# First token mixer reordered: u over half of the contraction, then v, then the rest of u, from one pool of tiles; the first norm and the spreading of a column redone

## The chip, the core and the metric

The kernel runs on one core of a Trainium2 chip. Time is device microseconds (us) of that core, the median of the runs shown. Five engines run in order, each with its own instruction stream: TensorE (PE, the matrix multiplier; PEld is its weight load), VectorE (DVE), ScalarE (ACT), GpSimd (POOL) and SyncE (SP, which issues most of the transfers from HBM). They wait for each other through semaphores. A scheduler in the language orders each engine's stream when the kernel is built; pools of tiles decide which instruction has to wait for a buffer.

## What is computed

Two layers over a sequence of 256 rows of 2048 features. Layer 0 mixes tokens with a chunked gMLP, layer 1 with attention; each is followed by a ConvFFN. The change is in layer 0's mixer:

```python
mod = silu(c) @ w_ada[i] + b_ada[i]              # 6 vectors of 2048 for each layer
sh1, sc1, gt1, sh2, sc2, gt2 = split(mod)
h = rmsnorm(x, g_norm) * (1 + sc1) + sh1
z = gelu(h @ w_in); u, v = split(z)              # w_in is 2048 x 4096
v = rmsnorm(v, g_v)
sv = einsum("gij,njgc->nigc", w_s, v) + b_s      # 16 groups, 2 chunks of 128 rows
x = x + gt1 * ((u * sv) @ w_out)
```

## The kernel before

Everything is float32, and each matrix product is split in three: an operand is cast to a rounded part (`hi`, on ACT) and a rest (`lo`, on DVE), and PE adds up hi*hi, hi*lo and lo*hi. A weight block is 1 MB, [128 x 2048]; `weight()` loads it into one of five `raw` buffers, casts it in two halves (L186) and subtracts in two halves (L187), into five buffers each for hi and lo. One block gives PE 48 matmuls of 256 columns, or 24 of 512.

The modulation is not a matmul. `ada()` (L135 to L143) loads 1 MB of `w_ada`, one vector of 128 outputs, into one of the same five `raw` buffers, and one DVE instruction (L138) multiplies it by the spread condition `cond_bc` and sums it up. There are 192 of these in the program. `queue` holds them in the order in which they are needed; `need()` forces those that the next step wants, and `pump()` takes as many more for each weight block as `state["rate"]` says.

The first mixer (`gmlp`, L296) does this: `rstd_bcast` forms the reciprocal norm of each row of x, and spreads it over the partitions: DVE writes it into a diagonal matrix (`dg`, L252) which PE multiplies by ones. The v half of `w_in` then runs with the contraction outermost: for each of 16 blocks kb, two `ada` (SC1 and SH1 of kb), the weight block, the modulated input (`make_h`: `ht` and `hlo` on DVE, `hhi` on ACT), and 24 matmuls into eight PSUM banks `pv`. After it v is squashed and normed. The u half runs by output block: 16 blocks `pu`, each with the whole contraction, which needs all of h; two of them stand ahead of the gating matmuls `pg` (32 of 128x128, operands `ws` and `bs` of 1 MB each), 14 behind. Then 16 output blocks `po` with `w_out`, each followed by the residual (L292). The ConvFFN begins with a norm of the new x and its first matmuls `pfa`.

## Time and profile before

| | |
|---|---|
| median of 3 runs | 2160.53 us (2158.19 to 2160.58) |
| the profiled execution | 2160.85 us, of which 2158.9 us are its span |
| PE busy | 2086.4 us, 97% of the span |
| DVE busy | 1704.8 us, 79% |
| ACT busy | 1020.2 us, 47% |
| moved by DMA | 580.62 MB, mean 269 GB/s |
| granted TensorE clock, mean | 0.983 of full speed |

The span runs from the first instruction to the last. Busy time is the time in which an engine executes an instruction; matmuls overlap each other, so a busy PE is not yet a PE at its peak. A start-to-start distance within a stream of equal instructions is the pace of the engine.

### The profile page before, as it was taken

The page shows a single profiled execution, that of the slowest core. Times are in us where ns is not written, and L with a number is a line of the kernel's source. Part 1 is how long each engine was busy: PE and PEld are TensorE (multiplying, and loading weights), DVE is VectorE, ACT ScalarE, POOL GpSimd, SP SyncE. Part 2 cuts the span into 40 slices and gives each one's busy share as a digit, 9 for nine tenths or more (in the row PEclk, how much of TensorE's full clock was granted, in tenths as well). Part 3 has the DMA queues.
Part 4 walks back from the last instruction along what each step waited for, and adds up shares of the span by engine and source line. Part 5 has one row for each costly group of instructions (what it writes and reads, how often), then busy time and mean ns, then how long its engine had stood idle before and what let it go on. Part 6 is the DMA issues. An engine that isn't in the chain of part 4 may idle for free.

```text
span 2158.9 us, 39151 instructions
## 1 busy us (share of the span) xinstructions
PE 2086.4 (97%) x16328; PEld 2020.9 (94%) x16328; DVE 1704.8 (79%) x2291; ACT 1020.2 (47%) x1501; POOL 16.6 (1%) x15
## 2 busy tenths in 40 slices
PE   6889998999999999999999999899999999999997
PEld 4669998999999999999988789899999999999997
DVE  8989888899988989889985677876978666655665
ACT  3354443446544554345455554443753455434542
POOL 0000000000000000000000000000000000000000
PEclk8999999999999999999999999899999999999999
DMA  9999987995798889888966346578558655555542
GB/s 381 400 378 372 347 334 278 335 363 206 286 362 332 330 320 344 336 324 316 341 244 214 117 176 236 218 283 296 197 179 318 229 191 180 192 182 189 178 159 94
DMA packets 85137, 580.62 MB, mean 269 GB/s; under 512 B 9952, under 2 KB 11488, under 8 KB 25056
## 3 DMA queue, kind: packets, MB, share of 16 engines
q1 hardware_dynamic: 84960, 578.12, 72.0%
q8 instruction: 128, 2.10, 0.4%
q14 instruction: 49, 0.40, 0.0%
HBM read 575.99 MB, written 2.10 MB: 268 GB/s over the span
## 4 chain that ended last, share of the span: by engine, by line
PE 55%; issue 36%; DVE 7%; ACT 1%; POOL 0%; DMA 0%; SPq 0%; POOLq 0%; DVEq 0%; ACTq 0%
PE pf L203 18%; PE pd L203 11%; PE po L203 4%; PE pw L203 4%; PE pu L203 4%; PE pfc L203 4%; PE pk L203 3%; DVE ada L138 3%; PE pq L203 3%; DVE lo L187 2%; PE pfa L203 2%; PE pqo L507 1%; PE pv L203 1%; PE psc L478 0%; ACT hi L186 0%
## 5 line engine op out<-in xcount | busy, mean ns | idle before, releaser
L186 ACT CAST hi<-w 128x1024 fp32r<-128x1024 f32 x740 | 741.0, 1009 | 916.6 <-PE pf L203 348.5
L187 DVE TENSOR_TENSOR lo<-w,hi 128x1024 fp32r<-128x1024 f32 x740 | 857.9, 1169 | 329.9 <-ACT hi L186 326.3
L203 PE MATMUL pf<-hhi_f,hi 128*128 128x256 f32 x2144 | 604.4, 282 | 0.0
L203 PE MATMUL pf<-hhi_f,lo 128*128 128x256 f32 x2144 | 601.2, 280 | 0.0
L203 PE MATMUL pf<-hlo_f,hi 128*128 128x256 f32 x2144 | 600.9, 280 | 0.0
L138 DVE CUSTOM_DVE_ANT_0 ada<-ada,cond_bc,bada 128x2048 f32<-128x2048 f32 x192 | 449.2, 2345 | 42.6 <-DMA ada<-in_wada 42.5
L203 PEld LDWEIGHTS pf<-hlo_f,hi 128*128 128x128 f32 x2144 | 404.8, 189 | 0.0
L203 PEld LDWEIGHTS pf<-hhi_f,lo 128*128 128x128 f32 x2144 | 404.3, 189 | 0.0
L203 PEld LDWEIGHTS pf<-hhi_f,hi 128*128 128x128 f32 x2144 | 403.8, 188 | 0.0
L203 PE MATMUL pd<-fhi_f,lo 128*128 128x256 f32 x1408 | 394.7, 281 | 0.0
L203 PE MATMUL pd<-flo_f,hi 128*128 128x256 f32 x1408 | 393.3, 280 | 0.0
L203 PE MATMUL pd<-fhi_f,hi 128*128 128x256 f32 x1408 | 391.1, 279 | 0.0
L203 PEld LDWEIGHTS pd<-fhi_f,hi 128*128 128x128 f32 x1408 | 264.8, 189 | 0.0
L203 PEld LDWEIGHTS pd<-fhi_f,lo 128*128 128x128 f32 x1408 | 264.7, 188 | 0.0
L203 PEld LDWEIGHTS pd<-flo_f,hi 128*128 128x128 f32 x1408 | 264.6, 188 | 0.0
L203 PE MATMUL pfc<-hhi_f,hi 128*128 128x256 f32 x448 | 125.3, 281 | 0.0
L203 PE MATMUL pfc<-hlo_f,hi 128*128 128x256 f32 x448 | 125.0, 281 | 0.0
L203 PE MATMUL pfc<-hhi_f,lo 128*128 128x256 f32 x448 | 124.4, 281 | 0.0
L571 DVE SCALAR_TENSOR_TENSOR t<-pf,cw,t 128x255 f32<-128x255 f32 x240 | 101.7, 474 | 0.0
L203 PEld LDWEIGHTS pfc<-hlo_f,hi 128*128 128x128 f32 x448 | 84.2, 188 | 0.0
L203 PEld LDWEIGHTS pfc<-hhi_f,lo 128*128 128x128 f32 x448 | 84.2, 189 | 0.0
L203 PEld LDWEIGHTS pfc<-hhi_f,hi 128*128 128x128 f32 x448 | 84.1, 188 | 0.0
(187 smaller groups left out, 2838.3 us busy)
## 6 DMA issues: line engine op xcount, KB each, us to landing
ada<-in_wada SPq DMA_DIRECT2D x192, 1024.0 KB, 6.6
w<-in_wup SPq DMA_DIRECT2D x134, 1024.0 KB, 4.9
w<-in_wdn SPq DMA_DIRECT2D x64, 1024.0 KB, 4.9
w<-in_wup SPq DMA_DIRECT2D x48, 896.0 KB, 5.9
w<-in_wdn SPq DMA_DIRECT2D x32, 768.0 KB, 4.6
w<-in_wv SPq DMA_DIRECT2D x16, 1024.0 KB, 6.9
w<-in_wu SPq DMA_DIRECT2D x16, 1024.0 KB, 7.2
w<-in_wout SPq DMA_DIRECT2D x16, 1024.0 KB, 5.2
```

What stands on the lines that cost most here:

```text
L138: V.tensor_tensor_reduce(out=w, in0=w, in1=cond_bc, op0=ALU.mult, op1=ALU.add, scale=1.0, scalar=bada[:, l, m:m + 1], accum_out=mod[:, l, ...
L186: A.copy(hi[:, :n], w[:, c:c + n])
L187: V.tensor_tensor(out=lo[:, :n], in0=w[:, c:c + n], in1=hi[:, :n].bitcast(F32), op=ALU.subtract)
L203: T.matmul(out, lhsT=a, rhs=b, start=start, stop=stop, skip_group_check=True)
L507: T.matmul(po, lhsT=va[:, kc, g * P:(g + 1) * P], rhs=ps_[h][:, kc, :], start=kc == 0, stop=kc == TC - 1)
L571: V.scalar_tensor_tensor(out=o[:, to], in0=a[:, frm], scalar=cw[:, l, tap, n:n + 1], in1=o[:, to], op0=ALU.mult, op1=ALU.add)
```

## The change

The u half of `w_in` is cut in two along the contraction. The mixer now runs:

1. u over the contraction blocks 0 to 7, contraction outermost, into eight banks `pua` (each holds two output blocks). Each block still comes with two `ada` and one `make_h`. The eight banks are copied to SBUF by ACT (`us`).
2. v over all 16 blocks. h of blocks 0 to 7 is there; blocks 8 to 15 are made on the way, with `ada` pumped at a rate of `RV` = 1.1 for each block.
3. the other half of u, by output (`u_rest`, eight blocks of two outputs each, added to `us` by DVE); the gating matmuls stand behind four of them. The rate is `RG` = 0.5.
4. the output blocks, as before, with a rate of `RO` = 1.15 in place of 0.7.

The number of weight blocks, `ada` and matmuls stays. v, u, sv and y now come in tiles of 512 columns from one pool of 20 slots (`slot`), and `ws` and `bs` have tiles of their own and no longer take `raw` buffers. A column is spread by one matmul whose stationary operand repeats it (`spread`), in place of a diagonal matrix; all four later norms use it too. The first sum of squares is four wide squares and three adds. `ident`, `bada` and `gn` are issued from ACT's queue; `gf`, `gv`, `cw` and `cb` stand in `late()`, behind the first stage in the code. The h tiles of the two mixers lose their padding of 8 columns.

```diff
-RO = 0.7
+RO = 1.15
+RV = 1.1
+RG = 0.5
+SVAT = 4
+HS = 20
...
+    ident = small("ident", [P, P], ident_d, A)
     x = const.tile([P, NB, S], F32, tag="x", name="x")
     for j in range(0, NB, 4):
         Q.dma_start(x[:, j:j + 4, :], xT_d[:, j:j + 4, :])
-    gf = small("gf", [P, NB], gf_d)
-    gv = small("gv", [P, NB], gv_d)
-    cw = small("cw", [P, DEPTH, 3, 2 * NPAIR], cw_d)
-    cb = small("cb", [P, DEPTH, 2 * NPAIR], cb_d)
...
+    bada = small("bada", [P, DEPTH, 6 * NB], bada_d, A)
+    gn = small("gn", [P, DEPTH * 2, NB], gn_d, A)
...
-    for b in range(NB // 2):
+    def spread(out, col):
+
+        T.matmul(out, lhsT=col.broadcast_to([P, P]), rhs=ident, start=True, stop=True)
+
+    for b in range(NB // 4):
         pb = bank(f"cb{b}")
-        dg = tmp.tile([P, S], F32, tag="ht", name=f"dgc{b}")
-        for i in range(2):
-            j = 2 * b + i
-            V.tensor_scalar(out=dg[:, i * P:(i + 1) * P], in0=ident, scalar1=cond[:, j:j + 1],
-                            scalar2=None, op0=ALU.mult)
-        T.matmul(pb[:, :S], lhsT=ones, rhs=dg, start=True, stop=True)
-        A.copy(cond_bc[:, b * S:(b + 1) * S], pb[:, :S])
+        for i in range(4):
+            spread(pb[:, i * P:(i + 1) * P], cond[:, 4 * b + i:4 * b + i + 1])
+        A.copy(cond_bc[:, b * 512:(b + 1) * 512], pb)
...
-        dg = tmp.tile([P, S], F32, tag="ht", name=f"dg_{name}")
...
-                V.tensor_scalar(out=dg[:, t * P:(t + 1) * P], in0=ident, scalar1=r[:, t:t + 1],
-                                scalar2=None, op0=ALU.mult)
-                T.matmul(pr[:, t * P:(t + 1) * P], lhsT=ones, rhs=dg[:, t * P:(t + 1) * P], start=True, stop=True)
+                spread(pr[:, t * P:(t + 1) * P], r[:, t:t + 1])
...
+    def new_h(name, step=0):
+        hts["hi"] = hbuf.tile([P, NB, S + step], F32R, tag="hhi", name=f"hhi_{name}")[:, :, :S]
+        hts["lo"] = hbuf.tile([P, NB, S + step], F32R, tag="hlo", name=f"hlo_{name}")[:, :, :S]
...
+    def late():
+
+        for t, src in ((gf, gf_d), (gv, gv_d), (cw, cw_d), (cb, cb_d)):
+            Q.dma_start(t, src)
...
-            gm = phase(st, "gm", NB)
+            gm = phase(st, "gm", 1)
             R = rstd()
             hhi, hlo = new_h("a")
-            v = gm.tile([P, TC, D], F32, tag="v", name="v")
-            pv = [[bank(f"pv{t}_{n}") for n in range(4)] for t in range(TC)]
-            for kb in range(NB):
+
+            def slot(name, dtype=F32):
+
+                return gm.tile([P, 2 * S + STEP], dtype, tag="half", name=name, bufs=HS)[:, :2 * S]
+
+
+            def h_block(kb):
                 need(l, SC1, kb)
                 need(l, SH1, kb)
+
+
+            pu = [bank(f"pua{i}") for i in range(H)]
+            for kb in range(H):
+                h_block(kb)
+                w = weight(wu0_d[kb], 2048)
+                make_h("a", l, 0, R, kb)
+                for i in range(H):
+                    for s in range(2):
+                        prod_b(pu[i][:, s * S:(s + 1) * S], w((2 * i + s) * P, P), hhi[:, kb, :], hlo[:, kb, :],
+                               kb == 0 and s == 0, kb == H - 1)
+            us = [slot(f"us{i}") for i in range(H)]
+            for i in range(H):
+                A.copy(us[i], pu[i])
+            late()
+
+
+            pv = [[bank(f"pv{t}_{n}") for n in range(4)] for t in range(TC)]
+            state["rate"] = RV
+            for kb in range(NB):
+                if kb >= H:
+                    h_block(kb)
                 w = weight(wv_d[kb], 2048)
-                make_h("a", l, 0, R, kb)
+                if kb >= H:
+                    make_h("a", l, 0, R, kb)
                 for t in range(TC):
                     ts_ = slice(t * P, (t + 1) * P)
                     for n in range(4):
...
                         mm(pv[t][n], hhi[:, kb, ts_], w(n * 512, 512)[1], False, False)
                     for n in range(4):
                         mm(pv[t][n], hlo[:, kb, ts_], w(n * 512, 512)[0], False, kb == NB - 1)
-            state["rate"] = 1.0
+            state["rate"] = RG
...
-                    vs = v[:, t, n * 512:(n + 1) * 512]
-                    A.activation(vs, pv[t][n], AF.Gelu)
-                    s = gm.tile([P, 512], F32, tag="vsq", name=f"vsq{t}{n}", bufs=2)
-                    A.activation(s, vs, AF.Square, accum_out=ss[:, t, n:n + 1])
+                    A.activation(v[t][n], pv[t][n], AF.Gelu)
+                    A.activation(slot(f"vsq{t}{n}"), v[t][n], AF.Square, accum_out=ss[:, t, n:n + 1])
...
+            for n in range(4):
+                for t in range(TC):
...
+                    V.tensor_scalar(out=v[t][n], in0=v[t][n], scalar1=rv[:, t:t + 1], scalar2=None, op0=ALU.mult)
+            ws = gm.tile([P, D], F32, tag="ws", name="ws")
+            Q.dma_start(ws, wsT_d)
+            bs = gm.tile([P, D], F32, tag="bs", name="bs")
+            Q.dma_start(bs, bs_d.partition_broadcast(P))
...
+            def u_rest(i):
+
+                w = weight(wu1_d[i], 2048)
+                pb = bank(f"pub{i}")
+                for s in range(2):
+                    for k in range(NB - H):
+                        prod_b(pb[:, s * S:(s + 1) * S], w((s * (NB - H) + k) * P, P), hhi[:, H + k, :],
+                               hlo[:, H + k, :], k == 0 and s == 0, k == NB - H - 1)
+
+                def fin():
+                    V.tensor_tensor(out=us[i], in0=pb, in1=us[i], op=ALU.add)
+                    A.activation(us[i], us[i], AF.Gelu)
+                    if i in sv:
+                        y_of(i)
+
+                pend.append(fin)
...
+            def sv_of(i):
+
+                pg = bank(f"pg{i}")
+                sv[i] = slot(f"sv{i}")
...
+            def y_of(i):
+                V.tensor_tensor(out=us[i], in0=us[i], in1=sv[i], op=ALU.mult)
+                hi, lo = slot(f"yhi{i}", F32R), slot(f"ylo{i}", F32R)
+                A.copy(hi, us[i])
+                V.tensor_tensor(out=lo, in0=us[i], in1=hi.bitcast(F32), op=ALU.subtract)
+                for s in range(2):
+                    ys[2 * i + s] = (hi[:, s * S:(s + 1) * S], lo[:, s * S:(s + 1) * S])
+
+            for i in range(SVAT):
+                u_rest(i)
             flush()
-            ws = raw_tile("ws")
-            Q.dma_start(ws, wsT_d)
-            bs = raw_tile("bs")
-            Q.dma_start(bs, bs_d.partition_broadcast(P))
-            for g in range(NB):
-                gsl = slice(g * P, (g + 1) * P)
-                pg = bank(f"pg{g}")
-                for t in range(TC):
-                    T.matmul(pg[:, t * P:(t + 1) * P], lhsT=v[:, t, gsl], rhs=ws[:, gsl],
-                             start=True, stop=True)
-                V.scalar_tensor_tensor(
-                    out=v[:, :, gsl], in0=pg[:, :S].rearrange("p (t i) -> p t i", t=TC),
-                    scalar=gv[:, g:g + 1], in1=bs[:, gsl].unsqueeze(1).broadcast_to([P, TC, P]),
-                    op0=ALU.mult, op1=ALU.add)
-            sv_ready.append(True)
-            for j in range(2):
-                y_of(j, us[j])
-            for j in range(2, NB):
-                u_block(j)
+            for i in range(H):
+                sv_of(i)
+            for i in range(SVAT):
+                y_of(i)
+            for i in range(SVAT, H):
...
 
-    for j in range(NB):
-        square_into("mx0", j, x[:, j, :])
+    quads = []
+    for j in range(0, NB, 4):
+        q = los.tile([P, 4 * S], F32, tag="lo", name=f"quad{j}")
+        A.activation(q, x[:, j:j + 4, :].rearrange("p j t -> p (j t)"), AF.Square)
+        quads.append(q)
+    for a, b in ((0, 1), (2, 3), (0, 2)):
+        V.tensor_tensor(out=quads[a], in0=quads[a], in1=quads[b], op=ALU.add)
+    accs["mx0"] = [quads[0][:, k * S:(k + 1) * S] for k in range(4)]
     gmlp(0, lambda: rstd_bcast("mx0", True))
...
-    o["wu"] = _nblock(win[:, :D])
+    wu = win[:, :D].reshape(2, NB // 2, P, NB // 2, 2, P)
+    o["wu0"] = win[:D // 2, :D].reshape(NB // 2, P, D)
+    o["wu1"] = wu[1].transpose(2, 1, 3, 0, 4).reshape(NB // 2, P, D)
```

SP's queue at the start, before; `ada` and `w` are 1 MB each, `w<-in_wv` are weight blocks of v:

```order
L97 DMA x<-in_xT 128x1024 x4
L88 DMA gf<-in_gf 128x16
L88 DMA gv<-in_gv 128x16
L88 DMA cw<-in_cw 128x528
L88 DMA cb<-in_cb 128x176
L137 DMA ada_16_223<-in_wada 128x2048
L137 DMA ada_0_227<-in_wada 128x2048
L180 DMA w_230<-in_wv 128x2048
L137 DMA ada_17_268<-in_wada 128x2048
L137 DMA ada_1_272<-in_wada 128x2048
L180 DMA w_275<-in_wv 128x2048
```

The same place after; `w<-in_wu` are the blocks of u's first half:

```order
L99 DMA x<-in_xT 128x1024 x4
L139 DMA ada_16_177<-in_wada 128x2048
L139 DMA ada_0_181<-in_wada 128x2048
L182 DMA w_184<-in_wu 128x2048
L139 DMA ada_17_246<-in_wada 128x2048
L139 DMA ada_1_250<-in_wada 128x2048
L297 DMA gf<-in_gf 128x16
L297 DMA gv<-in_gv 128x16
L297 DMA cw<-in_cw 128x528
L297 DMA cb<-in_cb 128x176
L361 DMA ws<-in_wsT 128x2048
L363 DMA bs<-in_bs 128x2048
L182 DMA w_253<-in_wu 128x2048
```

`ws` and `bs`, which stood behind the 18th weight block, now stand ahead of the second one.

DVE in the first mixer, one contraction block before (`ISA` is the `ada` instruction and its read-out):

```order
L138 ISA ada_3_362,mod<-ada_3_362,cond_bc,bada 128x2048
L138 ISA mod 128x1
L142 SCALAR_TENSOR_TENSOR gs<-mod,gn 128x1
L275 SCALAR_TENSOR_TENSOR ht_a_375<-x,gs,R_mx_210 128x256
L187 TENSOR_TENSOR lo_0_368<-w_365,hi_0_367 128x1024
L187 TENSOR_TENSOR lo_1024_372<-w_365,hi_1024_371 128x1024
L278 SCALAR_TENSOR_TENSOR hlo_a<-ht_a_375,mod,hhi_a 128x256
L138 ISA ada_20_403,mod<-ada_20_403,cond_bc,bada 128x2048
L138 ISA mod 128x1
L138 ISA ada_4_407,mod<-ada_4_407,cond_bc,bada 128x2048
L138 ISA mod 128x1
L142 SCALAR_TENSOR_TENSOR gs<-mod,gn 128x1
```

and in the middle of v after:

```order
L140 ISA ada_9_870,mod<-ada_9_870,cond_bc,bada 128x2048
L140 ISA mod 128x1
L277 SCALAR_TENSOR_TENSOR hlo_a<-ht_a_1116,mod,hhi_a 128x256
L189 TENSOR_TENSOR lo_0_876<-w_873,hi_0_875 128x1024
L189 TENSOR_TENSOR lo_1024_880<-w_873,hi_1024_879 128x1024
L140 ISA ada_26_907,mod<-ada_26_907,cond_bc,bada 128x2048
L140 ISA mod 128x1
L144 SCALAR_TENSOR_TENSOR gs<-mod,gn 128x1
L274 SCALAR_TENSOR_TENSOR ht_a_1157<-x,gs,R_mx_165 128x256
L189 TENSOR_TENSOR lo_0_914<-w_911,hi_0_913 128x1024
L189 TENSOR_TENSOR lo_1024_918<-w_911,hi_1024_917 128x1024
L140 ISA ada_10_945,mod<-ada_10_945,cond_bc,bada 128x2048
```

Two `ada` for each pair of `lo` and one `ht` and `hlo` have become one `ada` for each pair, and one `ht` and `hlo` for two pairs.

DVE at the end of u's second half and the start of the output blocks, after; `us_733` to `us_736` are the last four u tiles, `ylo` is the rest part of their products, which the output matmuls read:

```order
L375 TENSOR_TENSOR us_736<-pub_1989,us_736 128x512
L189 TENSOR_TENSOR lo_0_2179<-w_2176,hi_0_2178 128x1024
L140 ISA ada_41_2238,mod<-ada_41_2238,cond_bc,bada 128x2048
L140 ISA mod 128x1
L189 TENSOR_TENSOR lo_1024_2183<-w_2176,hi_1024_2182 128x1024
L402 TENSOR_TENSOR us_735<-us_735,sv_1740 128x512
L405 TENSOR_TENSOR ylo_1920<-us_734,yhi_1919 128x512
L189 TENSOR_TENSOR lo_0_2244<-w_2241,hi_0_2243 128x1024
L140 ISA ada_42_2301,mod<-ada_42_2301,cond_bc,bada 128x2048
L140 ISA mod 128x1
L402 TENSOR_TENSOR us_736<-us_736,sv_1748 128x512
L189 TENSOR_TENSOR lo_1024_2248<-w_2241,hi_1024_2247 128x1024
L405 TENSOR_TENSOR ylo_1986<-us_735,yhi_1985 128x512
```

The adds, products and subtractions of the last u tiles stand between `lo` and `ada` of the output blocks.

## Rows read from the trace of the kernel before

**Rows 1.** Profile page, busy time of PE: us, share of the span, instructions.
```profile
PE 2086.4 (97%) x16328; PEld 2020.9 (94%) x16328; DVE 1704.8 (79%) x2291; ACT 1020.2 (47%) x1501; POOL 16.6 (1%) x15
```

**Rows 2.** Windows: stretch, length, busy PE, PEld, DVE, ACT, POOL, then PEclk, DMA share, GB/s.
```profile
31.30:147.20 115.90, 101.00 (x384) 75.71 (x385) 115.16 (x134) 40.45 (x49) 0.00 (x0) 0.94 1.01 403
147.20:249.30 102.10, 99.57 (x835) 98.53 (x834) 92.42 (x114) 48.99 (x84) 0.70 (x1) 1.00 0.90 356
249.30:339.40 90.10, 90.10 (x769) 90.10 (x768) 77.52 (x89) 39.53 (x44) 0.00 (x0) 1.00 0.87 330
...
350.00:375.00 25.00, 25.00 (x207) 25.00 (x207) 21.03 (x30) 11.27 (x16) 0.00 (x0) 0.97 0.68 254
```

**Rows 3.** Timeline of PE: start, duration, instruction; first u, last output, first ConvFFN matmul.
```profile
147.21 0.28 PE L203 MATMUL pu<-hhi_a,hi 128*128 128x256 f32 x1
...
339.33 0.28 PE L203 MATMUL po<-fhi_y,lo 128*128 128x256 f32 x1
...
348.50 0.80 PE L203 MATMUL pfa<-hhi_f,hi 128*128 128x256 f32 x2 [1.52 <-ACT hhi_f L277]
```

**Rows 4.** Timeline of DVE: one contraction block of v.
```profile
132.28 0.48 DVE L275 SCALAR_TENSOR_TENSOR ht_a<-x,gs,R_mx 128x256 f32<-128x256 f32 x1
132.68 2.35 DVE L187 TENSOR_TENSOR lo<-w,hi 128x1024 fp32r<-128x1024 f32 x2
134.95 0.48 DVE L278 SCALAR_TENSOR_TENSOR hlo_a<-ht_a,mod,hhi_a 128x256 fp32r<-128x256 f32 x1
135.34 2.35 DVE L138 CUSTOM_DVE_ANT_0 ada<-ada,cond_bc,bada 128x2048 f32<-128x2048 f32 x1
...
137.61 2.35 DVE L138 CUSTOM_DVE_ANT_0 ada<-ada,cond_bc,bada 128x2048 f32<-128x2048 f32 x1
...
140.08 0.48 DVE L275 SCALAR_TENSOR_TENSOR ht_a<-x,gs,R_mx 128x256 f32<-128x256 f32 x1
```

**Rows 5.** The chain that ended last: start, duration, what; block 7 of v.
```profile
78.06 2.35 DVE lo L187 x2
```

**Rows 6.** DMA by slices of 1.5 us from the start (view of transfers, 0 to 60).
```profile
GB/s 0 65 200 216 412 347 380 428 426 426 426 421 421 415 426 426 426 421 421 415 426 426 421 415 421 410 431 421 410 388 404 410 399 415 404 399 377 371 382 393
```

**Rows 7.** Timelines of SP's queue and ACT: issues of x, ws, bs; third weight block.
```profile
2.59 1.86 SPq L97 DMA_DIRECT2D x<-in_xT  x4
...
142.86 0.33 SPq L359 DMA_DIRECT2D ws<-in_wsT  x1
145.53 0.33 SPq L361 DMA_DIRECT2D bs<-in_bs  x1
...
34.66 1.05 ACT L186 CAST hi<-w 128x1024 fp32r<-128x1024 f32 x1 [3.00 <-DMA w<-in_wv]
```

**Rows 8.** Groups of DVE from 147 to 340: count, busy us, mean ns.
```profile
L368 DVE SCALAR_TENSOR_TENSOR v<-pg,gv,bs 128x256 f32<-128x256 f32 x16 | 6.6, 475 | 0.0
...
L233 DVE TENSOR_TENSOR acc_ff<-acc_ff,sq_ff 128x512 f32<-128x512 f32 x6 | 4.1, 684 | 0.0
L328 DVE TENSOR_SCALAR v<-v,rv 128x2048 f32<-128x2048 f32 x2 | 2.5, 1283 | 0.8 <-POOL rv L326 0.8
```

**Rows 9.** Timelines of DVE, POOL and PE at the norm ahead of the ConvFFN.
```profile
340.72 0.48 DVE L292 SCALAR_TENSOR_TENSOR x<-po,mod,x 128x256 f32<-128x256 f32 x1
342.41 0.16 DVE L249 TENSOR_SCALAR r_ff<-pm_ff 128x2 f32<-128x2 f32 x1
345.41 0.48 DVE L252 TENSOR_SCALAR dg_ff<-ident,r_ff 128x128 f32<-128x128 f32 x2 [0.58 <-POOL r_ff L250]
...
342.64 2.73 POOL L250 TENSOR_TENSOR r_ff<-r_ff,neghalf 128x2 f32<-128x2 f32 x1 [184.63 <-DVE r_ff L249]
...
345.75 1.22 PE L254 MATMUL pr_ff<-dg_ff,ones 128*128 128x128 f32 x4 [3.39 <-DVE dg_ff L252]
```

**Rows 10.** Timeline of PE: first matmuls of v.
```profile
31.91 0.63 PE L203 MATMUL pv<-lo,hhi_a 128*128 128x512 f32 x1
31.91 0.33 PEld L203 LDWEIGHTS pv<-hi,hhi_a 128*128 128x128 f32 x1
32.34 0.63 PE L203 MATMUL pv<-hi,hhi_a 128*128 128x512 f32 x1
```

65 lines of the change are left out of this document (26 added, 39 removed).

## The prediction, made before the changed kernel ran

> **What bounds the kernel now.** I read the page first: PE is busy for 97% of the span [rows 1], so only the places where PE is not at its pace can pay. Then I cut the first mixer into windows [rows 2]. From 147.2 to 339.4 us (the rest of u, the gating, the output blocks) PE is busy for 99.57 of 102.1 and 90.10 of 90.1 us, at full clock: 769 matmuls in 90.1 us are 0.1172 us each, so a weight block of 48 costs 5.63 us. A v block streams the same columns in 24 wide matmuls, and I give it the same 5.63 us. From 31.3 to 147.2, the v half, it is different. Its 16 blocks are 16 x 5.63 = 90.1 us of PE work and take 115.9 us, while DVE is busy for 115.16 us. The timeline of DVE shows why [rows 4]: between one `ht` (132.28) and the next (140.08) lie 7.80 us, with no gap: two `ada` at 2.27 us from start to start (135.34 to 137.61), two `lo` in 2.27 (132.68 to 134.95), `hlo` and `ht` at 0.40, and the small instruction on the gain. So in v DVE sets 7.80 us for each block where PE needs 5.63. DMA moves three 1 MB tiles in that time, at 403 GB/s [rows 2], and is about level with it. So the excess comes from the `ada`, two for each block, because all 32 must be done within 16 blocks. From 339.33 to 348.50 [rows 3] PE waits for the norm.
>
> **What the change does.** It spreads those 32 `ada` over 24 blocks. I divide the new run at one point: the end of stage 1 on PE (u over blocks 0 to 7), called T.
>
> *Behind T.* PE has 16 blocks of v (90.1 us) and then what stood behind v before, 192.2 us (147.2 to 339.4), less the eight u blocks now done, 45.0 us. That is 237.3 us, if nothing else waits; the 2.5 us for which PE idled between 147.2 and 249.3 [rows 2] are kept in it. Does DVE keep up? In v it has 16 pairs of `lo` (36.3 us), 17 `ada` (38.6) and eight `ht` and `hlo` (6.4) with their gains: 83 us against 90.1. From the start of v to the last output block I count 40 `ada` (90.8), 40 pairs of `lo` (90.8), 6.4 for h, 24 passes over 512 columns for the adds, products and rests of u (nearest row 0.684 [rows 8], 16.4), 16 gatings at 0.475 (7.6), the norming of v (2 x 1.28), 16 residuals at 0.48 [rows 9], six sums at 0.684, some 5 us of small ones: 231 us against 237 for PE. It fits, with little to spare. Does DMA? v takes 33 tiles of 1.049 MB, 34.6 MB in 90.1 us, 384 GB/s; the output blocks 34 tiles, 396 GB/s; the trace held 403 for 116 us and 421 to 426 in its best slices [rows 6]. It fits, narrowly.
>
> Adds that lie beside other work: the eight copies of `pua` and the casts on ACT, 40% busy in the output stage [rows 2]; the first banks are copied while PE is at the last ones. The last u tiles become y in DVE's order between `lo` and `ada` (the last order piece): from the last add to the last rest lie about 15 us of DVE's queue, and meanwhile PE has 174 matmuls of the output blocks that need only the earlier y (20.6 us, counted in its order). If that cover went, it would cost up to 15 us; I price it at nothing, and the rival on DVE below holds it.
>
> *T itself.* Stage 1 has DVE's 7.80 us per block as before, so T follows from when block 1 can begin. Before, `lo` of block 7 began at 78.06 [rows 5]. In SP's queue the four small loads, `ws` and `bs` now stand ahead of the second weight block (second order piece), and whatever SP holds back waits behind them: that block, then all later ones. Before, `ws` and `bs` were issued at 142.86 and 145.53 [rows 7], where u had already begun to be PE's. They are 2.1 MB, 5.0 us of a stream that was full from about 5 us on (412 to 428 GB/s [rows 6]). Before, the third weight block was cast at 34.66, released by its DMA [rows 7]. It was the ninth 1 MB tile. The second block is now the eighth: 2.5 us earlier, and 1.4 us more because x (issued at 2.59 [rows 7]) no longer stands behind three loads: about 30.8. Cast, then `lo` at 31 to 31.8; I take 31.0. Six periods of 7.80 later `lo` of block 7 begins at 77.8, its `hlo` ends at 80.5, and PE has 40 of its 48 matmuls left behind it (4.7 us): T = 85.3. So the earlier start that the new norm allows is eaten by `ws` and `bs`; the norm and the spreading at the start are worth nothing, since DVE and PE wait for the second block. Bounds: if the two loads cost nothing, DVE could reach block 1 about 4 us sooner (27.5 by the sum of its own work), T = 82; if small loads and lost slices delay the stream by 3 us more, T = 89.
>
> *Later norms.* `spread` takes out the DVE step between the power and the matmul: 345.41 to 345.75, 0.34 us [rows 9]. Four norms: 1.4 us. At the ConvFFN's start the residual waited until 340.72 and the sum until 342.41 behind DVE's queue [rows 9]. After, an `ada` and two `lo` stand there too; I take no difference, bounds 2 us either way (the power alone took 2.73 us there). The ConvFFN begins with 56 `ada` done instead of 59: 6.8 us of DVE move into a stage where it has 4 us free in each 25 (21.03 busy [rows 2]); nothing. The missing padding of h: no row shows it; nothing, bounds 1 us either way.
>
> **The sum.** The last output matmul stood at 339.4 and now stands at T + 237.3 = 322.6: 16.8 us. With 1.4 us: 18.2. The profiled execution took 2160.85 us, 0.3 above the median: 2142.6 us.
>
> **A rule against it.** The trace sustains 403 GB/s over 116 us with one core running [rows 2]. The Trainium skill, "DMA: Bandwidth & Descriptors", section Specifications, states a limit of about 358 GB/s from HBM for one core. This trace disagrees: it is above that wherever the queue is full. By that figure three tiles would take an estimated 8.8 us, v 96.7 and the outputs 99.6, some 22 us more in all: 2165, level with before or slower.
>
> **Rivals.**
> - *The two loads are free* (they move beside the others at no cost). Speaks for it: slices of 426 [rows 6]. T = 82: 2139. Chance 0.13.
> - *DMA or DVE binds behind T.* If a full queue gives only what the later windows suggest (330 GB/s at a share of 0.87 is 379 [rows 2]), the outputs take 94 us, v 91.3 and stage 1 3 us more: 8 us lost; DVE with its 6 us of spare and the y chain can lose as much. Against it: 403 held before, and in 147 to 249 DVE was busy for 92.4 of 102 without PE losing more than 2.5. 2151. Chance 0.20.
> - *The other side: TensorE's clock in stage 1.* Each block of `pua` starts with eight matmuls when `hhi` is there and then waits for `hlo`, so PE stands still once more in each period. At the lower level, 1.2 GHz, the first v matmuls were 0.43 us apart (31.91 to 32.34 [rows 10]): 10.3 us for a block's columns, and with 0.33 us for each of 48 weight loads [rows 10] 15.8. Stage 1 would then go by PE: 8 x 2.5 = 20 us (2163, no change or a little slower) up to 64 us (2207). It decides from 10.1 us a block on. Against it: with similar waits the granted clock was 0.94 over the v stage [rows 2]. Chance 0.05.
> - *DMA holds all of it back.* If the stream gives no more than the 356 GB/s of the second window [rows 2], three tiles take 8.84 us, v 97.2 and the outputs 100.1: 6 + 7 + 10 = 23 us lost, 2166. It decides below about 360 GB/s. Against it: the share there was 0.90, so nobody asked for more, and the first window had 403. The limit in the Trainium skill, "DMA: Bandwidth & Descriptors", section Specifications, is this case. Chance 0.04.
> - The forecast, 2137 to 2148 by T from 83.5 to 87, 3 us of waits behind T and the norm's bounds: chance 0.58.
>
> **How the numbers follow.** A measurement of this kernel tells about 0.2% (4.3 us) from no change. The forecast and the first two rivals lie below 2156.2; half of the clock's and of the slow stream's chance lies within 0.2%, half above. Faster 0.91, same 0.05, slower 0.04. The range takes in the two rivals on the same side, 2134 (T = 82, a norm 2 us shorter, no new waits) to 2152; about 0.15 is left out.
>
> **What would show it.** After: `ws` and `bs` issued before 20 us and the second weight cast at 29 to 32; `lo` in stage 1 every 7.8 us; T at 83 to 88 (first `pv`); `pv` to `pub` 90 us later, with PE busy over 24.5 in 25; the last `po` at 320 to 326; `pfa` 8 to 10 us later. I am wrong if PE shows gaps between blocks of v (then DVE or DMA binds: whichever released it), if the clock in stage 1 falls below 0.9, or if `po` waits for DVE's `ylo`.

## The result and the profile after

The changed kernel takes 2148.22 us (median of 4 runs, 2147.55 to 2148.59), the kernel before beside it 2160.25 (2158.19 to 2160.58): a ratio of 0.9947, 95% interval 0.9935 to 0.9958, 12.0 us faster. The forecast was 18.2 us. Its profiled execution took 2148.5 us with a span of 2146.7, 12.2 less than before (2158.9). Where a stage begins is read from the first matmul of its accumulator in the trace (`pfa` and `pfc` belong to a ConvFFN's first pass and `pf` to the pass behind it; `pk`, `pq` and `pw` follow one another in the attention, `pw` being its output product):

| first or last matmul | before, us | after, us | gain so far | forecast |
|---|---|---|---|---|
| last `po` | 339.3 | 329.1 | 10.2 | 16.8 |
| first `pfa`, ConvFFN 0 | 348.5 | 338.0 | 10.5 | 17.1 |
| first `pf` | 469.2 | 464.8 | 4.4 | 17.1 |
| first `pk`, attention | 1104.8 | 1100.8 | 4.0 | 17.5 |
| first `pw` | 1281.8 | 1270.4 | 11.4 | 17.5 |
| first `pfa`, ConvFFN 1 | 1393.9 | 1381.9 | 12.0 | 17.8 |
| end of the span | 2158.9 | 2146.7 | 12.2 | 18.2 |

So the first mixer gave 10.2 us, three fifths of the 16.8 forecast for it. Then 6.1 us were lost in ConvFFN 0 and 7.4 won in the attention, two stages in which the diff changes next to nothing. All three places were opened with experiments.

Windows of the changed kernel, by stage: u over half, v, the rest of u with the gating, the output blocks. They answer to [rows 2].

```profile
core 0: us, PE busy (x) PEld busy (x) DVE busy (x) ACT busy (x) POOL busy (x), PEclk, DMA share, GB/s
31.00:87.30 56.30, 45.64 (x345) 43.23 (x344) 54.03 (x62) 20.66 (x27) 0.00 (x0) 0.97 1.01 420
87.30:179.60 92.30, 89.20 (x386) 71.09 (x385) 81.85 (x87) 39.41 (x51) 0.00 (x0) 1.00 0.96 370
179.60:236.70 57.10, 55.31 (x449) 54.91 (x449) 54.68 (x73) 31.89 (x48) 1.61 (x1) 0.97 0.77 286
236.70:329.20 92.50, 91.02 (x770) 90.72 (x769) 88.91 (x99) 39.14 (x45) 0.00 (x0) 1.00 0.95 361
```

DVE is the busy engine of stage 1 (54.03 of 56.3). In v it is busy for only 81.85 of 92.3 us, and PE for 89.20: neither is full, so something must be waited for in turn. DMA moved 420 GB/s for 56 us, and the granted clock was 0.97 in that window (0.93 from 23.5 us on, when PE starts): the rivals that stage 1 goes by the lower clock, and that DMA holds everything back, are out.

The timeline of SP's queue (start, duration, instruction), with the loads in the order that the prediction read:

```profile
14.78 0.33 SPq L361 DMA_DIRECT2D ws<-in_wsT  x1
17.27 0.33 SPq L363 DMA_DIRECT2D bs<-in_bs  x1
19.82 0.33 SPq L182 DMA_DIRECT2D w<-in_wu  x1
```

The timelines of ACT and DVE behind it, stage 1:

```profile
30.88 2.00 ACT L188 CAST hi<-w 128x1024 fp32r<-128x1024 f32 x2 [2.13 <-DMA w<-in_wu]
39.55 0.51 ACT L276 ACTIVATE hhi_a<-ht_a,mod 128x256 fp32r<-128x256 f32 x1 [6.67 <-DVE ht_a L274]
39.96 1.98 ACT L188 CAST hi<-w 128x1024 fp32r<-128x1024 f32 x2
```

```profile
31.95 2.36 DVE L189 TENSOR_TENSOR lo<-w,hi 128x1024 fp32r<-128x1024 f32 x2 [2.69 <-ACT hi L188]
...
41.02 2.36 DVE L189 TENSOR_TENSOR lo<-w,hi 128x1024 fp32r<-128x1024 f32 x2 [0.45 <-ACT hi L188]
...
48.44 2.35 DVE L189 TENSOR_TENSOR lo<-w,hi 128x1024 fp32r<-128x1024 f32 x2
...
79.64 2.35 DVE L189 TENSOR_TENSOR lo<-w,hi 128x1024 fp32r<-128x1024 f32 x2
```

The second weight block is cast at 30.88, released by its DMA (forecast 30.8), and `lo` of block 1 waits for that cast. The step from block 1 to 2 is 9.07 us, not 7.80: ACT's queue holds the weight cast of block 2 behind `hhi` of the same block, which waits for DVE's `ht`. From block 2 on the step is 7.4 to 7.8. First `pv` at 87.3 (forecast 85.3).

One period of v on DVE, two blocks in 11.4 us (one `ht` and `hlo` for two pairs of `lo`), answers to [rows 4]:

```profile
96.69 2.35 DVE L189 TENSOR_TENSOR lo<-w,hi 128x1024 fp32r<-128x1024 f32 x2
98.96 2.35 DVE L140 CUSTOM_DVE_ANT_0 ada<-ada,cond_bc,bada 128x2048 f32<-128x2048 f32 x1
101.23 0.08 DVE L140 DVE_READ_ACCUMULATOR2_ANT mod<- 128x1 f32 x1
101.90 0.48 DVE L277 SCALAR_TENSOR_TENSOR hlo_a<-ht_a,mod,hhi_a 128x256 fp32r<-128x256 f32 x1 [0.58 <-ACT hhi_a L276]
102.84 2.36 DVE L189 TENSOR_TENSOR lo<-w,hi 128x1024 fp32r<-128x1024 f32 x2 [0.46 <-ACT hi L188]
105.12 2.34 DVE L140 CUSTOM_DVE_ANT_0 ada<-ada,cond_bc,bada 128x2048 f32<-128x2048 f32 x1
```

The `ada` at 98.96 makes the shift of a block of h. ACT needs it for `hhi`, DVE needs `hhi` for `hlo`, and `hlo` stands next in DVE's queue: 0.58 us of waiting. ACT's next cast came behind that `hhi`, so `lo` waits 0.46 more. In all of v it is 7.2 us:

```profile
DVE hlo_a L277 <- ACT hhi_a L276: 4.0, 7, 0.6
DVE lo L189 <- ACT hi L188: 3.2, 7, 0.5
```

(columns: us in total, times, longest.)

PE's own pace is read where it has nothing to wait for. One block of v begins here, and then the next:

```profile
114.57 1.98 PE L205 MATMUL pv<-hi,hhi_a 128*128 128x512 f32 x8
...
120.01 1.98 PE L205 MATMUL pv<-hi,hhi_a 128*128 128x512 f32 x8
```

That is 5.44 us for 24 matmuls, 0.227 us each, so 10.9 us for two blocks. DVE's period of 11.40 us (91.44 to 102.84) is longer, but without its 1.04 us of waits it would be shorter. In v PE falls behind at 12 places, 4.1 us together.

### The profile page after: what moved, and what is told of

Its sections match the earlier page's. It is cut to its first block, busy times and chain, and to the rows that moved or that the text cites. A ratio compares the mean times of both kernels' runs of the same rounds, so it can differ in the third digit from the quotient of the medians.

```text
span 2146.7 us, 39158 instructions
## 1 busy us (share of the span) xinstructions
PE 2081.6 (97%) x16348; PEld 2026.0 (94%) x16348; DVE 1703.8 (79%) x2258; ACT 1018.3 (47%) x1484; POOL 17.4 (1%) x15
## 4 chain that ended last, share of the span: by engine, by line
PE 51%; issue 37%; DVE 7%; ACT 2%; DMA 2%; POOL 0%; SPq 0%; POOLq 0%; DVEq 0%; ACTq 0%
PE pf L205 18%; PE pd L205 12%; PE po L205 4%; DVE ada L140 3%; PE pw L205 3%; PE pk L205 3%; DVE lo L189 3%; PE pq L205 3%; PE pfc L205 3%; PE pfa L205 2%; PE pub L205 1%; ACT hi L188 1%; DMA w<-in_wu 1%; PE pqo L549 1%; DMA ada<-in_wada 1%
## 5 line engine op out<-in xcount | busy, mean ns | idle before, releaser
L205 PE MATMUL pfc<-hhi_f,lo 128*128 128x256 f32 x448 | 113.8, 282 | 0.0
L205 PEld LDWEIGHTS pfc<-hlo_f,hi 128*128 128x128 f32 x448 | 85.3, 190 | 2.0 <-DVE hlo_f L277 2.0
L205 PEld LDWEIGHTS pfc<-hhi_f,lo 128*128 128x128 f32 x448 | 79.9, 190 | 0.2 <-DVE lo L189 0.2
```

The source lines that it names most:

```text
L205: T.matmul(out, lhsT=a, rhs=b, start=start, stop=stop, skip_group_check=True)
```

## What was lost in ConvFFN 0: the `ada` that were missing

From the first `pfa` to the first `pf` the changed kernel takes 126.8 us, before 120.7. The timeline of DVE in the second half of `pfc`, where each new block of h needs its two `ada`:

```profile
435.21 2.35 DVE L140 CUSTOM_DVE_ANT_0 ada<-ada,cond_bc,bada 128x2048 f32<-128x2048 f32 x1
...
438.20 2.35 DVE L140 CUSTOM_DVE_ANT_0 ada<-ada,cond_bc,bada 128x2048 f32<-128x2048 f32 x1
...
440.47 2.35 DVE L140 CUSTOM_DVE_ANT_0 ada<-ada,cond_bc,bada 128x2048 f32<-128x2048 f32 x1
...
445.73 2.35 DVE L140 CUSTOM_DVE_ANT_0 ada<-ada,cond_bc,bada 128x2048 f32<-128x2048 f32 x1
...
448.00 2.35 DVE L140 CUSTOM_DVE_ANT_0 ada<-ada,cond_bc,bada 128x2048 f32<-128x2048 f32 x1
```

Two `ada` in a block of 7.53 us (440.47 to 448.00), where PE has 42 matmuls, 4.9 us at the pace of [rows 2]. The rate of 0.75 `ada` a block gives 56 + 16 x 0.75 = 68 by the middle of `pfc`; its blocks 8 to 15 need 66, 68, 70 ... 80. From the third of them on `need` has to force what is missing, so that two `ada` fall in every block. Windows of the second half of `pfc`: changed, before, and a kernel with the rates 0.75, 1.0 and 1.0 (its experiment stands below, with the attention):

```profile
421.00:464.80 43.80, 41.13 (x328) 40.37 (x327) 40.58 (x49) 16.53 (x23) 0.00 (x0) 0.96 0.96 361
```

```profile
430.00:469.20 39.20, 39.20 (x334) 39.20 (x333) 36.03 (x45) 16.89 (x23) 0.00 (x0) 1.00 0.98 395
```

```profile
421.00:460.50 39.50, 39.50 (x336) 39.50 (x335) 37.52 (x45) 18.81 (x24) 0.00 (x0) 1.00 1.01 411
```

In the changed kernel PE waits 2.7 us there for `hlo` and a cast, and the granted clock of the window is 0.96, not 1.00: behind the last of the waits the matmuls of 256 columns follow one another at 0.21 us and not 0.12, the lower of the clock's two levels (1.2 GHz). By an estimate from the window's clock, 43.8 x 0.04, that is 1.8 us more. The first experiment raises the rates, so that the 80 are there in time.

```diff
-RK = ((0.75, 0.75, 0.75, 0.0), (0.6, 0.6, 0.6, 0.0))
+RK = ((0.9, 1.05, 1.0, 0.0), (0.6, 0.6, 0.6, 0.0))
```

> The changed kernel with more `ada` in ConvFFN 0's first pass: the three rates there are 0.9, 1.05 and 1.0 for each weight block, not 0.75; nothing else differs. Theory (the three `ada` that are missing at the ConvFFN's start are asked for two at a time in blocks 11 to 15 of h, and PE waits there for DVE): at 0.9 to 1.05 all SC2 and SH2 are there before their blocks, the first pf comes 127 us after pfa (338 to 465) less 5 to 6 us, at about 459.5, and the time is 2142 to 2144. Rival (DVE and DMA have no room in the first pass, so the same wait moves ahead into pfa and the first half of pfc): first pf at 463 to 466, time 2146 to 2149.

First `pf` 121.6 us behind the first `pfa` (339.2 to 460.8), so the stage is nearly as it was before the change (120.7). Yet the time is 2149.67 us (5 runs, ratio 0.9951, interval 0.9939 to 0.9964), no better than the changed kernel. The stage moved as the theory said and the time as the rival said: the attention gave the gain back. From the first `pk` to the first `pw` it takes 174.4 us, in the changed kernel 169.6, before 177.0.

## What came back in the attention: order, clock, and the rows of h

The diff changes nothing in the attention but the padding of h (and the spreading in its norm). Two things were found there. First the padding.

```diff
-            hhi, hlo = new_h("b")
+            hhi, hlo = new_h("b", STEP)
```

> The changed kernel with the padding of 8 elements put back in the rows of the attention's h alone (as before the change). Theory (the stationary operand h without padding is what makes the 512-wide pk and pq matmuls faster, 389 ns instead of 394 in the mean, 41 instead of 40 in 8.9 us): 40 in 8.9 us again, the pk stage 1.9 us and the three q products 1.6 us longer, time 2151 to 2152, and up to 3.4 more if the attention's low clock stretches come back with it (2155). Rival (the gain in the attention comes from the time at which its waits fall, or from where the tiles lie in memory): pace unchanged at 41, 2148.

In the other direction, the kernel before with the padding taken out of both mixers:

```diff
-    def new_h(name):
+    def new_h(name, step=0):
...
-        hts["lo"] = hbuf.tile([P, NB, S + STEP], F32R, tag="hlo", name=f"hlo_{name}")[:, :, :S]
+        hts["lo"] = hbuf.tile([P, NB, S + step], F32R, tag="hlo", name=f"hlo_{name}")[:, :, :S]
...
-            hhi, hlo = new_h(f"f{l}")
+            hhi, hlo = new_h(f"f{l}", STEP)
```

> The kernel before with the padding taken out of the rows of h in both mixers, nothing else. Theory (padding): pk and pq matmuls at 41 in 8.9 us, 3.5 us less in the attention; v there is set by DVE at 7.80 us a block, so nothing is gained in it: 2156 to 2157. Rival (the pace came with the order or the place of the tiles): 2160.

The `pk` matmuls of the four kernels by tile (duration in ns, min/median/max, then first and last start): before, changed, changed with padding, before without.

```profile
L203 PE MATMUL pk<-lo,hhi_b x96: 387/395/628, 1105.4 to 1172.8; 128*128 128x512 f32 x96
```

```profile
L205 PE MATMUL pk<-lo,hhi_b x96: 389/389/628, 1101.4 to 1166.8; 128*128 128x512 f32 x96
```

```profile
L205 PE MATMUL pk<-lo,hhi_b x96: 387/394/628, 1100.2 to 1167.1; 128*128 128x512 f32 x96
```

```profile
L203 PE MATMUL pk<-lo,hhi_b x96: 389/389/628, 1107.4 to 1173.3; 128*128 128x512 f32 x96
```

The padding sets the pace, in both kernels: 394 or 395 ns with it, 389 without. (The ends of matmuls are modelled in a profile; the median distance from one start to the next says the same, 0.232 us with the padding and 0.227 without.) From the first `pk` to the first `pq` that is 69.0 (before), 67.0 (changed), 68.3 (padded again), 67.4 us (before without): 1.3 to 1.6 us. The `pq` matmuls have the same two paces, but between the first `pq` and the first `pw` the changed kernel takes 102.6 us with and without. The kernel before takes 108.0 with and 106.3 without; that this is the padding is not shown, since another kernel with it, the kernel before with the new start (below), takes 106.8. In the whole time it isn't resolved: 2149.62 us (0.9949, 0.9937 to 0.9962) and 2158.84 (0.9993, 0.9984 to 1.0002).

The rest is from the first `pq` to the first `pw`: 108.0 us before, 102.6 in the changed kernel, 106.5 in the first experiment, 102.6 padded again. The kernels fall into two groups by the order in which a scheduler put PE's and ACT's instructions there: before, its unpadded variant and the first experiment have one, word for word; the changed kernel and its padded variant have another, in which some transposes of `p` and products `pqo` stand 4 to 16 `pq` matmuls later. DVE's order differs too. What the order depends on is not in the attention: a rate in ConvFFN 0 is enough to turn it. So two kernels were made, the first for the gap in ConvFFN 0 under the changed kernel's order, the second for the kernel before in that order.

```diff
-RK = ((0.75, 0.75, 0.75, 0.0), (0.6, 0.6, 0.6, 0.0))
+RK = ((0.75, 1.0, 1.0, 0.0), (0.6, 0.6, 0.6, 0.0))
```

> The changed kernel with the first pass of ConvFFN 0 at rates of 0.75, 1.0 and 1.0 for the `ada`; of the rates that close the gap in pfc it is one that leaves PE, ACT in the attention in the order of the changed kernel (the rates of the first run put them in the order of the kernel before). Theory (two things were mixed in the first run: the closed gap, worth 5 us, and the attention's order, which took 3.9 back): the first pf at 459 to 461, from the first pq to the first pw 102.6 us, time 2143 to 2144.5. Rival (the attention gives back whatever is gained ahead of it, since it depends on when it begins): 106 to 108 us from pq to pw, time 2148 to 2150.

```diff
-RD = 0.85
+RD = 0.8
```

> The kernel before with one number changed: 0.8 `ada` for each output block of ConvFFN 0, not 0.85; PE and ACT in the attention then stand in the order of the changed kernel, and nothing in the first mixer moves. Theory (the attention's gain is that of its order): from the first pq to the first pw 103 to 104.5 us (102.6 and up to 1.6 for the padded h), not 108.0, time 2156 to 2157. Rival (the attention's gain comes from the change itself, the rows of h or the time): 108, 2160.

Both as the theory had it: 102.9 and 103.0 us from `pq` to `pw`. Over all fourteen kernels of this document, the four with the order of before take 106.3 to 108.0 us there, the ten with the other 102.4 to 103.0. The changed kernel with the gap closed takes 2143.49 us (5 runs; ratio 0.9921, 0.9909 to 0.9934). The kernel before in the other order has a span of 2154.1 us, 4.8 less; its median of 11 runs is 2158.13 (0.9988, 0.9979 to 0.9997), 2.4 less than that of before beside it, so the times carry half of what the two profiled executions show.

Where in the attention it lies is read from the windows around the second and third group's softmax. Before, then the kernel before in the other order, then the changed kernel (columns as above; the last but two is the granted clock; one line of the changed kernel, for the second place):

```profile
1198.00:1212.00 14.00, 11.02 (x44) 8.51 (x43) 8.61 (x27) 10.56 (x36) 1.64 (x1) 0.76 0.21 75
...
1244.00:1256.00 12.00, 9.71 (x37) 7.49 (x36) 6.37 (x15) 3.39 (x18) 1.64 (x1) 0.86 0.37 153
```

```profile
1199.00:1213.00 14.00, 10.95 (x50) 8.73 (x49) 10.24 (x30) 10.74 (x36) 1.64 (x1) 0.88 0.19 75
...
1245.00:1257.00 12.00, 12.00 (x57) 9.74 (x58) 8.74 (x14) 3.48 (x8) 1.64 (x1) 1.00 0.30 93
```

```profile
1236.00:1248.00 12.00, 11.70 (x53) 9.43 (x52) 8.61 (x16) 4.19 (x17) 1.64 (x1) 1.00 0.32 127
```

The same two places in the kernel before without the padding, which has the order of before:

```profile
1198.00:1212.00 14.00, 10.57 (x47) 8.32 (x46) 9.37 (x28) 10.74 (x36) 1.64 (x1) 0.88 0.21 75
...
1244.00:1256.00 12.00, 9.69 (x37) 7.62 (x37) 5.71 (x12) 2.97 (x16) 1.64 (x1) 0.86 0.31 128
```

And the wait at the second of these places, before and in the other order:

```profile
PE pq L203 <- ACT qsqq L426: 2.3, 1, 2.3
```

```profile
PE pq L203 <- ACT qsqq L426: 0.3, 1, 0.3
```

Before, PE stands for 2.3 us until ACT has squared the last q product, and the granted clock of that window is 0.86: soon behind the wait eight matmuls follow one another at 0.43 us and not 0.23, again the lower level. In the other order the wait is 0.3, the clock 1.00, and 57 matmuls stand in 12 us where 37 did. That makes 2.0 us of waiting and, estimated from the window's clock, 12 x 0.14 = 1.7 us: 3.7. All four kernels with the order of before have this wait of 2.3 us and this clock of 0.86; the ten others wait 0.3 us and have 1.00.

The first place is another matter. There the clock is 0.76 before and 0.88 in the other order, but 0.88 as well in two kernels with the order of before, the unpadded one above and the one with the new start. So it does not go with the order. At like padding the order alone is worth 3.4 to 3.8 us: 106.3 against 102.9 without the padding (before unpadded, and the changed kernel with the gap closed), 106.8 against 103.0 with it (before with the new start, and before in the other order). The other 1.2 of the 5.0 us between before and before in the other order go with the first place's clock, and what sets that clock is open: the first experiment has 0.76 there too and takes only 106.5.

## Why v and the outputs took longer than forecast

Two kernels take from `ada` in v and in the output stage either half of DVE's work or half of the bytes: the first sums only half of the columns, the second loads only half and sums it twice. Neither forms the whole modulation, so only the stages' times are read.

```diff
+        n = D // 2 if state["cut"] else D
         Q.dma_start(w, wada_d[l, m])
-        V.tensor_tensor_reduce(out=w, in0=w, in1=cond_bc, op0=ALU.mult, op1=ALU.add, scale=1.0,
+        V.tensor_tensor_reduce(out=w[:, :n], in0=w[:, :n], in1=cond_bc[:, :n], op0=ALU.mult, op1=ALU.add, scale=1.0,
                               scalar=bada[:, l, m:m + 1], accum_out=mod[:, l, m:m + 1])
```

> The changed kernel with `ada` in v and in the output stage summed over half of its columns (the whole tile is still loaded; the modulation comes out wrong): 1.1 us less of DVE each, DMA as it was. Theory (v and the output blocks lose 2 us each against PE's pace to DVE): from first pv to first pub 85 to 88 us (PE's 24 matmuls at 0.217 us are 5.21 a block, 83.4), from first to last po 89 to 90.2. Rival (DMA sets the pace there): 92 and 92 as in the changed kernel.

```diff
+        n = D // 2 if state["cut"] else D
-        Q.dma_start(w, wada_d[l, m])
+        Q.dma_start(w[:, :n], wada_d[l, m][:, :n])
+        for _ in range(D // n):
+            V.tensor_tensor_reduce(out=w[:, :n], in0=w[:, :n], in1=cond_bc[:, :n], op0=ALU.mult, op1=ALU.add,
+                                   scale=1.0, scalar=bada[:, l, m:m + 1], accum_out=mod[:, l, m:m + 1])
```

> The changed kernel with half a tile loaded for each `ada` in v and in the output stage, and summed twice (the modulation comes out wrong): DVE as before, a quarter less for DMA in v. Theory (DVE): from first pv to first pub 91 to 92.5, from first to last po 92. Rival (DMA): 85 to 88, and 89 to 90.2.

From the first `pv` to the first `pub`: 88.4 us with half the sums, 87.1 with half the loads, 92.7 in the changed kernel. Each looks like its own proof, so the two did not tell DVE from DMA by that number: in both PE ran without a gap (86.8 us from the first to the last `pv`, no two starts more than 0.24 us apart); beyond that neither number can tell what held PE back before. Other rows do. With half the sums DMA moved 407, 422 and 420 GB/s in the windows from 87.3 to 156 us, where the changed kernel had 379, 357 and 370: the queue could have given more than it was asked for. And half the loads put DVE's instructions in another order, in which no `hlo` waits in v, with DVE busy for all of 110 to 156. Its first `pv` came 4.3 us late (91.6): the last `hlo` of stage 1 stood behind half an `ada`, 1.8 us later, and the matmuls behind it took 7.4 us at a granted clock of 0.61 (4.9 at 1.00 in the changed kernel). So v ended at 178.5 as in the changed kernel. What was left as suspect was the wait itself. The next experiment takes it away alone, on top of the rates 0.75, 1.0 and 1.0, by asking for the shift of a block ahead of its scale, so that two `lo` stand between `ht` and `hlo`:

```diff
-        queue.extend([(0, SC1, j), (0, SH1, j)])
+        queue.extend([(0, SH1, j), (0, SC1, j)])
```

> The kernel with rates 0.75, 1.0, 1.0 in ConvFFN 0, and the first mixer's `ada` asked for with the shift ahead of the scale for each block of h; the same instructions, and the attention in the order of the changed kernel. Between ht and hlo of a block in v DVE now has two lo, where it had the ada whose result ACT needs for hhi, so hlo no longer waits for ACT. Theory (v's 2 us over the forecast are DVE's waits for ACT, 7.2 us in 91): those waits fall below 2 us, PE's own pace of 5.21 us a block shows further into v, the first pub comes 2 to 4 us earlier (89 to 91 us after the first pv, not 92.7), time 2140 to 2142. Rival (without the waits the next thing in v, DMA or DVE's work itself, holds the pace): first pub within 1 us of where it was, 2143 to 2144.

DVE's waits from 88 to 180 us in this kernel:

```profile
DVE lo L189 <- ACT hi L188: 7.9, 3, 6.9
DVE hlo_a L277 <- ACT hhi_a L276: 0.6, 1, 0.6
```

The 6.9 is one wait at the end of v (172.0 to 178.9), where DVE has run out of work early; `hlo`'s are down from 4.0 to 0.6 us. v takes 88.4 us (90.5 to 178.9), not 92.7. The kernel started 1.3 us later than the one that it edits (first `pua` 25.0 and 23.7), its stage 1 has a step of 7.93 us between blocks, and the first `pub` still comes 2.6 us earlier than without the edit (181.5). Windows of v, as above, and below them one of the changed kernel:

```profile
87.30:110.00 22.70, 22.70 (x112) 19.34 (x112) 22.56 (x25) 14.03 (x19) 0.00 (x0) 0.99 1.01 401
110.00:133.00 23.00, 23.00 (x103) 19.04 (x102) 22.82 (x26) 8.56 (x10) 0.00 (x0) 1.00 1.01 415
133.00:156.00 23.00, 23.00 (x103) 19.06 (x102) 21.82 (x25) 10.78 (x13) 0.00 (x0) 1.00 0.98 383
```

```profile
133.00:156.00 23.00, 21.07 (x90) 15.99 (x88) 21.08 (x24) 8.04 (x10) 0.00 (x0) 1.00 0.96 370
```

PE now runs 103 matmuls in 23 us without a gap, 86.8 us from the first `pv` to the last as with half the sums and half the loads: v goes by PE. DVE, almost full at first, is ahead of it at the end. The time is 2141.16 us (5 runs; 0.9912, 0.9898 to 0.9925), the fastest of all; against the 2143.49 of the kernel that it edits the intervals overlap, so the 2.6 us are shown in the stage and not in the whole.

In the output stage the loss is mostly one place, near the end. DVE's and PE's timelines of the changed kernel:

```profile
322.03 0.48 DVE L291 SCALAR_TENSOR_TENSOR x<-po,mod,x 128x256 f32<-128x256 f32 x1 [2.24 <-PE po L205]
322.43 2.35 DVE L189 TENSOR_TENSOR lo<-w,hi 128x1024 fp32r<-128x1024 f32 x2
```

```profile
323.70 0.38 PE L205 MATMUL po<-yhi,lo 128*128 128x256 f32 x1 [1.48 <-DVE lo L189]
```

DVE holds a residual at the head of its queue and idles 2.24 us until PE has finished that block; the `lo` for PE's next block stands behind it, though its weights were cast by 319.5. PE then waits 1.48 us for this `lo`. Half the sums leave the wait (92.2 us from first to last `po`), half the loads, with their other order, don't have it (90.6).

## The two early loads, and the new start

The prediction charged `ws` and `bs` for the late start. They were held back, by one column copied into each tile from a late block of h ahead of the load:

```diff
             ws = gm.tile([P, D], F32, tag="ws", name="ws")
+            A.copy(ws[:, :1], hhi[:, NB - 1, :1].bitcast(F32))
             Q.dma_start(ws, wsT_d)
```

(and the same for `bs`).

> The changed kernel with the two loads ws and bs held back to the last h block of v (a copy of one column of hhi into each tile ahead of its DMA). Theory (they stand ahead of the second weight block, which is what lo of block 1 waits for): the second block lands 4 to 5 us sooner, lo of block 1 starts when DVE is done with its own work at about 29.3, not 31.95, the first pv stands at 84 to 85 instead of 87.3, and all behind it moves as well: 2145 to 2146. If the wait of block 2 (9.07 instead of 7.80 us) goes too, 2144.5. Rival (v takes what it takes from DMA, so the start doesn't matter, or the two loads delay the u rests when they come later): first pv earlier, last po still at 329, 2148.

`lo` of block 1 starts at 30.92, now behind an ACT cast that waits for DVE and not for a DMA; the first experiment, whose first instructions came as late, has it at 33.17. So the 2.25 us are there at that point. But the first `pv` is at 87.7, the first `pub` at 179.1, and the two loads now stand between the first and second rests of u: the last `pub` comes at 240.9 (236.6 in the changed kernel), the last `po` at 333.2. 2151.11 us (5 runs; 0.996, 0.9947 to 0.9972). Put into v, on top of the rates 0.75, 1.0 and 1.0:

```diff
+            A.copy(ws[:, :1], hhi[:, 8, :1].bitcast(F32))
             Q.dma_start(ws, wsT_d)
```

> The fastest kernel so far (rates 0.75, 1.0, 1.0 in ConvFFN 0) with ws and bs held back to the ninth h block, so that they are issued between the second and third tiles of v rather than ahead of the second weight block or ahead of the rests of u; the attention's order is that of the changed kernel. Theory (in v DMA moves 370 GB/s where 407 to 422 were had with shorter sums, so it can carry the two loads beside the rest): 2.3 us gained at the start stay, 2141 to 2142. Rival (the two loads take the place of tiles that DVE then waits for, 5 us of the stream): 2143.5 to 2147.

First `pv` 2.1 us earlier (86.7, not 88.8), first `pub` level (181.7 and 181.5): PE's waits for ACT's casts in v rise from 1.5 to 3.2 us. The span is 2141.6 and 2141.3 us; the medians 2141.95 (0.9916, 0.9901 to 0.993) and 2143.49 don't tell the two apart. Three places, and nowhere did moving the 2 MB make the whole measurably faster.

The start alone (with the new order of the first loads, not shown) and the spreading, in the kernel before:

```diff
-    for j in range(NB):
-        square_into("mx0", j, x[:, j, :])
+    quads = []
+    for j in range(0, NB, 4):
+        q = los.tile([P, 4 * S], F32, tag="lo", name=f"quad{j}")
...
-                T.matmul(pr[:, t * P:(t + 1) * P], lhsT=ones, rhs=dg[:, t * P:(t + 1) * P], start=True, stop=True)
+                spread(pr[:, t * P:(t + 1) * P], r[:, t:t + 1])
```

> The kernel before with only the new start (the order of the first loads, the four-block squares of the first norm) and the spreading without the diagonal step, in all norms; both mixers as before, and PE and ACT in the attention in the order of before. Theory (the new start is worth nothing in the changed kernel because ws and bs then stand ahead of the second weight block; without them there it is worth what the second block comes earlier): lo of block 1 at 29 to 30 us, the first mixer 2 to 4 us earlier up to po, and about 0.3 us for each later norm: 2155.5 to 2157.5. Rival (start and spreading are worth nothing anywhere, all of the gain is the reordered mixer): 2159.5 to 2160.5.

No difference: 2159.39 us (12 runs; 0.9997, 0.9987 to 1.0006). The theory fell: `lo` of block 1 starts at 29.80, but before it started at 30.53 already, and the 9.01 us to block 2 take that back (block 7 at 77.44 and 78.06). DVE's own work, not a load, set the start there. And the spreading:

```diff
-                spread(pr[:, t * P:(t + 1) * P], r[:, t:t + 1])
+                V.tensor_scalar(out=dg[:, t * P:(t + 1) * P], in0=ident, scalar1=r[:, t:t + 1],
+                                scalar2=None, op0=ALU.mult)
+                T.matmul(pr[:, t * P:(t + 1) * P], lhsT=ones, rhs=dg[:, t * P:(t + 1) * P], start=True, stop=True)
```

> The changed kernel with the DVE step of the old spreading back in the five norms (diagonal of the inverse root, then a matmul with ones); cond is still spread the new way. Theory (0.34 us in each of four norms, and the first one is hidden): 2149.6, and 0.3 to 0.4 us more from the last output block to the first pfa. Rival (the step costs nothing, or more than its time since DVE's queue stands before it): 2148.2, or over 2151.

Inconclusive: 2150.7 us (6 runs; 0.9954, 0.994 to 0.9968), an interval that overlaps the changed kernel's, with a span of 2147.2 us against 2146.7. From the last `po` to the first `pfa` both take 8.9 us; ahead of ConvFFN 1, from the last `pw` to the first `pfa`, it is 12.8 against 11.5.

## Why the prediction was right, and where its terms were off

The direction and the place were right: v at 7.80 us a block went by DVE's `ada`, and spread over 24 blocks they let PE run. The time lies in the range, 5.6 us over the forecast. That it is so near is luck: it is the sum of larger errors, two of them in opposite directions. Of the prediction's own signs the first `pv` came as forecast (87.3), but PE had gaps in v and the last `po` stood at 329.1, not 320 to 326.

- **T, 85.3 forecast, 87.3 measured (-2.0).** The step by which `ws` and `bs` hold back the second weight block was right to 0.1 us (cast at 30.88). `lo` came 1 us behind it, and one of the "six periods of 7.80" took 9.07 by an order on ACT that the period read from v doesn't have. That the start is worth nothing was right (2159.39 alone); that the loads' place decides it was only half right, since no other place made the kernel faster.
- **"16 blocks of v (90.1 us)", measured 92.7 (-2.6).** Two sizes were off in opposite ways. PE's pace for the wide matmuls without the padding is 5.44 us a block, not 5.63: 87.1 us. (In the kernel before, with it, they follow one another at 0.233 us, 5.6 a block, so the forecast's figure was near that kernel's. The 0.217 us and the 5.21 us a block of two expectations above stand in no trace.) To the 87.1 come 4.1 us of gaps and 1.5 from the last `pv` to the first `pub`. "83 us against 90.1" counted DVE's work, which it has (81.85), but not the waits for ACT inside its own queue, 7.2 us. The order piece for the middle of v had `hlo` next to the `ada` it depends on. The rival that DVE binds behind T is, with these waits, what happened; that DMA binds is refuted, since with half the sums and with the swapped pair it moved 401 to 422 GB/s in windows where the changed kernel had 357 to 379.
- **The rest of u and the gating: 57.1 forecast, 56.7 measured.** Right. **The outputs: 90.1 forecast, 92.4 measured (-2.3),** of which 1.5 us are the one wait of PE for `lo`. The 15 us of cover for the last y held.
- **"56 `ada` instead of 59 ... nothing" (-6.1).** This step failed. Room in DVE's mean (4 us in each 25) says nothing of a deadline: the three were due at blocks of h that take two each, at a rate that never made them up. 120.7 us became 126.8; the first experiment took 121.6, the changed kernel with the gap closed 121.1.
- **The attention, not in the sum but for 1 us either way of the padding (+7.4).** 2.0 us of it lie from `pk` to `pq`, 1.3 to 1.6 of them the padding; 5.4 lie from `pq` to `pw`, where the instructions' order alone is worth 3.4 to 3.8; of the rest some 1.2 go with a lower clock in the kernel before, whose cause is open. The bounds of 1 us for the padding were a little narrow, its gain of 0.006 us a matmul in v was not seen, and the order was not thought of. The order of the attention could have been compared beforehand; the prediction looked only at the first mixer.
- **The norms, 1.4 us:** 0.3 us at the first, 0.6 at ConvFFN 1, and not resolved in the whole.

From 18.2: less 2.0, 2.6, 2.3 and 6.1, plus 0.4 and 7.4, is 13.0; the remaining 0.8 lies mostly between the first `pf` and the first `pk`, where 0.4 us were forecast as gained and 0.4 were lost (12.2 measured). Without the attention's gain the change would have been worth about 5 us, some 2156, and the forecast would have missed its range.

The Trainium skill ("DMA: Bandwidth & Descriptors", section Specifications) gives about 358 GB/s from HBM as the limit for one core, which it has by dividing a stack's rate between two cores. Here one core ran, and it moved 420 GB/s over 56 us of stage 1: the measurement decides, and this row of the page is not a bound for a core that runs alone.

## What to carry to other kernels

When work is moved out of a stage, list for each later consumer by when it is due and at what rate it is made up: a mean of free time hides a deadline. Where a queue runs in order, count the waits inside it, not only its work: an instruction that needs an answer from another engine should have something independent between question and answer, and here it took one swapped pair to get it. And a scheduler's order is part of the change: compare it over the whole program, since here a rate in one stage moved another by over 3 us.
